# An expert-dispatch kernel on one core: eight groups of 16 tokens in place of nine groups of 15 and 14, with the last group also stored in two pieces

## The chip, the cores and the metric

The kernel runs on one core of a Trainium2 chip, with the other cores idle. The metric is the device time of one execution in microseconds (us). The kernel before takes 242.47 us, the median of three runs (242.39 to 246.49).

## What is computed

Each of 16 x 1024 tokens is a row of 512 float32 numbers. The reference repeats the row k = 2 times and multiplies each copy by one of the token's two weights. The expert indices are not used.

```python
x_expanded = x[:, :, np.newaxis, :].repeat(k, axis=2)      # (16, 1024, 2, 512)
weights = expert_weights[..., np.newaxis]                  # (16, 1024, 2, 1)
return (x_expanded * weights).astype(np.float32)
```

33.6 MB are read, 67.1 MB are written, and one multiplication is made for each number written.

## The kernel before

The 16,384 tokens are spread over 128 partitions, 128 tokens on each, and worked off in groups. A group of T takes 128 x T neighbouring tokens; partition p holds T tokens that lie next to each other in memory (`rows`), so that one partition's share of a load is one run of T x 2 KB and of a store one run of T x 4 KB. `groups` (line 30) is [15, 15, 14, 14, 14, 14, 14, 14, 14].

**Slots.** There are three slots (`slots`, bufs=3), each as large as the output of the largest group. Input and output share a slot: `load` (lines 112 to 124) puts the input into the last half of the part that the group uses, and the products are written from the front. `ranges` (lines 127 to 135) cuts a group so that no product overwrites input that is still needed: the first VectorE instruction takes about half of the tokens, the next half of what is left, and so on, down to all tokens but the last. `products` (line 140) is one VectorE multiplication with both weights of each token broadcast along the row. The last token's two products are made by ScalarE in `last` (line 157), since their place is that of the input itself.

**Weights.** The weights are loaded in long rows by `weights_in` (line 68, on the SP queue) and spread over the partitions by `weights_spread`: TensorE transposes blocks of columns (line 84), VectorE copies them out in another order (line 89), TensorE transposes back (line 95), and VectorE writes `w_tile` (line 100). Since a weights load has the same group size throughout, there are two: one for the two groups of 15, one for the seven groups of 14. Every product needs the `w_tile` columns of its group.

**Order.** The order of the work is the order of the program on each engine (a manual schedule). All token loads are issued on the ScalarE queue, all stores and the weights loads on the SP queue. At the start the two weights loads and the loads of groups 0, 1 and 2 are issued; the load of group 0 is two transfers of 7 and 8 tokens. Then, for each group: the VectorE products, the two ScalarE products, and the store (line 184). For group 0 alone, the output of the first VectorE product is stored on its own as soon as it is there (line 180), and the rest by line 184. After group i (from group 1 on) the load of group i + 2 is issued; it goes into the slot of group i - 1, and so waits until the store of that group has landed. It waits on the ScalarE queue, behind the two products of group i and ahead of those of group i + 1.

Of the kernel before, what the change touches and what calls it, by code (L numbers as in the profile page):

```python
# [1 line left out]

# [4 lines left out]


@with_exitstack
def kernel(  # L10
    ctx: ExitStack,
    tc: tile.TileContext,
    x: bass.AP,
    expert_indices: bass.AP,
    expert_weights: bass.AP,
    out: bass.AP,
):
    nc = tc.nc

    batch, seq, hidden = x.shape  # L20
    k = expert_weights.shape[-1]
    P = nc.NUM_PARTITIONS
    ntok = batch * seq
    assert ntok % P == 0

    f32 = mybir.dt.float32
    row = k * hidden


    groups = [15, 15, 14, 14, 14, 14, 14, 14, 14]  # L30
    assert sum(groups) * P == ntok
    TX = max(groups)

    xf = x.rearrange("b s h -> (b s) h")
    of = out.rearrange("b s k h -> (b s) (k h)")
    wf = expert_weights.rearrange("b s k -> (b s) k")

    w_pool = ctx.enter_context(tc.tile_pool(name="w_pool", bufs=1))
    slots = ctx.enter_context(tc.tile_pool(name="slots", bufs=3))
    raw_pool = ctx.enter_context(tc.tile_pool(name="raw_pool", bufs=1))  # L40
    psum = ctx.enter_context(
        tc.tile_pool(name="psum", bufs=2, space=bass.MemoryType.PSUM)
    )

    w_tile = w_pool.tile([P, sum(groups) * k], f32)

    def rows(flat, done, T):
        return flat[done * P : (done + T) * P, :].rearrange("(p a) n -> p (a n)", a=T)

    B = 8
    M = P // B
    ident = w_pool.tile([P, P], f32)
    nc.gpsimd.memset(ident, 0.0)  # L55
    nc.gpsimd.affine_select(  # L56
        out=ident,
        in_=ident,
        compare_op=mybir.AluOpType.not_equal,
        fill=1.0,  # L60
        base=0,
        pattern=[[-1, P]],
        channel_multiplier=1,
    )

    def weights_in(head, G, T):
        raw_tile = raw_pool.tile([G * M, B * T * k], f32, name=f"raw{T}_tile")
        nc.sync.dma_start(  # L68
            out=raw_tile,
            in_=wf[head * P : (head + G * T) * P, :].rearrange(  # L70
                "(q a) n -> q (a n)", a=B * T
            ),
        )
        return raw_tile

    def weights_spread(raw_tile, head, G, T):
        n = T * k
        col_tile = raw_pool.tile([n, G * P], f32, name=f"col{T}_tile")
        cols = col_tile.rearrange("c (q r) -> c q r", r=B)
        step = 4  # L80
        for r0 in range(0, B, step):
            up_tile = psum.tile([n, step, G * M], f32)
            for r in range(step):
                nc.tensor.transpose(  # L84
                    up_tile[:, r, :],
                    raw_tile[:, (r0 + r) * n : (r0 + r + 1) * n],
                    ident[: G * M, : G * M],
                )
            nc.vector.tensor_copy(  # L89
                out=cols[:, :, r0 : r0 + step],  # L90
                in_=up_tile.rearrange("c r q -> c q r"),
            )
        down_tile = psum.tile([P, G * n], f32)
        for g in range(G):
            nc.tensor.transpose(  # L95
                down_tile[:, g * n : (g + 1) * n],
                col_tile[:, g * P : (g + 1) * P],
                ident[:n, :n],
            )
        nc.vector.tensor_copy(  # L100
            out=w_tile[:, head * k : (head + G * T) * k], in_=down_tile
        )

    ctx.enter_context(tc.manual_schedule())

    starts = [sum(groups[:i]) for i in range(len(groups))]
    loaded = []

    def load(i):
        if i >= len(groups):
            return
        T = groups[i]
        slot_tile = slots.tile([P, TX * row], f32)
        loaded.append(slot_tile)
        src = rows(xf, starts[i], T)
        at = T * (row - hidden)
        for lo, hi in [(0, T // 2), (T // 2, T)] if i == 0 else [(0, T)]:  # L120
            nc.scalar.dma_start(
                out=slot_tile[:, at + lo * hidden : at + hi * hidden],
                in_=src[:, lo * hidden : hi * hidden],
            )


    def ranges(T):
        lo, out = 0, []
        while lo < T - 1:
            hi = lo + 1  # L130
            while (hi + 1) * k <= T * (k - 1) + lo and hi < T - 1:
                hi += 1
            out.append((lo, hi))
            lo = hi
        return out

    def products(slot_tile, T, lo, hi, w_at):
        m = hi - lo
        at = T * (row - hidden) + lo * hidden
        nc.vector.tensor_tensor(  # L140
            out=slot_tile[:, lo * row : hi * row].rearrange(
                "p (t k h) -> p t k h", t=m, k=k
            ),
            in0=slot_tile[:, at : at + m * hidden]
            .rearrange("p (t h) -> p t h", t=m)
            .unsqueeze(2)
            .to_broadcast([P, m, k, hidden]),
            in1=w_tile[:, w_at + lo * k : w_at + hi * k]
            .rearrange("p (t k) -> p t k", t=m)
            .unsqueeze(3)  # L150
            .to_broadcast([P, m, k, hidden]),
            op=mybir.AluOpType.mult,
        )

    def last(slot_tile, T, w_at):
        for c in range(T * k - k, T * k):
            nc.scalar.mul(  # L157
                out=slot_tile[:, c * hidden : (c + 1) * hidden],
                in_=slot_tile[:, T * row - hidden : T * row],
                mul=w_tile[:, w_at + c : w_at + c + 1],  # L160
            )

    raw15 = weights_in(0, 2, 15)
    raw14 = weights_in(30, 7, 14)
    load(0)
    load(1)
    load(2)
    weights_spread(raw15, 0, 2, 15)
    weights_spread(raw14, 30, 7, 14)

    for i, T in enumerate(groups):
        slot_tile = loaded[i]
        outr = rows(of, starts[i], T)
        w_at = starts[i] * k
        done = 0
        for lo, hi in ranges(T):
            products(slot_tile, T, lo, hi, w_at)
            if i == 0 and done == 0:
                done = hi
                nc.sync.dma_start(  # L180
                    out=outr[:, : done * row], in_=slot_tile[:, : done * row]
                )
        last(slot_tile, T, w_at)
        nc.sync.dma_start(
            out=outr[:, done * row :], in_=slot_tile[:, done * row : T * row]
        )
        if i:
            load(i + 2)

# [1 line left out]
_INS = ['x', 'expert_indices', 'expert_weights']  # L191
_OUTS = [((16, 1024, 2, 512), 'float32')]


# [23 lines left out]
```

## Time and profile before

| | before |
|---|---|
| median of the runs | 242.47 us (242.39, 242.47, 246.49) |
| profiled execution, its own time | 242.25 us |
| span of that execution, from first to last instruction | 240.4 us |
| moved by DMA | 100.80 MB |
| loads of x | 10 transfers, ScalarE queue (q10) |
| stores | 10 transfers, SP queue (q1, with 2 loads of weights) |

All numbers of the trace come from the one profiled execution. The span is 1.85 us shorter than its time. An instruction group's line gives, after the shapes and the count, the busy time in us and the mean ns of one instruction, and then the idle time ahead of it with what ended most of it. In the table of stretches (start:end in us, length) the engines' busy times are followed by the granted TensorE clock (1.00 throughout), the mean busy share of the 16 DMA engines, and the GB/s moved; a DMA packet is counted whole where it starts, so short stretches can stand above 1.00 or too low. "DMA to landing" is the time from the issue of a transfer until its completion is seen. In the chain of waits a line is: start, length, what ran or was waited for.

### The profile page before, as it was taken

Reading aid. Unit: us, or ns where it says so; the run is one execution under the profiler, and the core shown is the slowest. Engines: PE = TensorE matmul, PEld = TensorE weight load, DVE = VectorE, ACT = ScalarE, POOL = GpSimd, SP = SyncE. Lnnn points to the kernel's source line nnn. Section 1 sums busy time; section 2 is a strip of 40 time slices with the busy share of each in tenths; the row PEclk is TensorE's granted clock in tenths of the full one; section 3 lists DMA queues with packets and bytes.
Section 4 is the critical chain, followed back from the end, with each engine's and each line's share of the span. In section 5 each row is a group of like instructions: output and inputs, shape, how many; then the busy total and the mean of one; then the engine's idle time right before and its main releaser. Section 6 shows DMA issues by size and latency. Waiting matters only on the chain.

```text
span 240.4 us, 221 instructions
## 1 busy us (share of the span) xinstructions
PE 3.6 (1%) x25; PEld 2.5 (1%) x25; DVE 134.7 (56%) x42; ACT 14.3 (6%) x19; POOL 0.7 (0%) x6
## 2 busy tenths in 40 slices
PE   1210000000000000000000000000000000000000
PEld 1110000000000000000000000000000000000000
DVE  1189999998000697079605980399019930895000
ACT  0020010200100002000200011000200020002000
POOL 1000000000000000000000000000000000000000
DMA  7999999999799899899999997998999998897897
GB/s 268 464 434 392 382 458 414 436 491 480 316 480 458 382 458 458 382 448 391 458 525 391 458 458 310 453 458 386 453 458 458 458 458 382 382 458 305 363 401 305
DMA packets 3056, 100.80 MB, mean 419 GB/s; under 512 B 352, under 2 KB 496, under 8 KB 496
## 3 DMA queue, kind: packets, MB, share of 16 engines
q1 hardware_dynamic: 1616, 67.24, 64.7%
q10 hardware_dynamic: 1440, 33.56, 32.9%
HBM read 33.69 MB, written 67.11 MB: 419 GB/s over the span
## 4 chain that ended last, share of the span: by engine, by line
DMA 57%; DVE 31%; ACT 2%; PE 1%; issue 1%; SPq 0%; DVEq 0%
DVE slot_tile L140 31%; DMA out_dram<-slot_tile 29%; DMA slot_tile<-in_x_dram 24%; DMA raw_tile<-in_expert_weights_dram 4%; ACT slot_tile L157 2%; PE up_tile L84 1%; PE down_tile L95 0%; DVE col_tile L89 0%; SPq L68 0%; DVEq L140 0%; DVE w_tile L100 0%
## 5 line engine op out<-in xcount | busy, mean ns | idle before, releaser
L140 DVE TENSOR_TENSOR slot_tile<-slot_tile,w_tile 128x7168 f32<-128x7168 f32 (+4 forms) x36 | 132.5, 3684 | 73.4 <-DMA slot_tile<-in_x_dram 72.5
L157 ACT ACTIVATE slot_tile<-slot_tile,w_tile 128x512 f32<-128x512 f32 x18 | 13.0, 721 | 194.2 <-DVE slot_tile L140 193.9
L89 DVE COPY col_tile<-up_tile 30x128 f32<-30x128 f32 (+1 forms) x4 | 1.7, 445 | 10.0 <-PE up_tile L84 9.9
L84 PE MATMUL up_tile<-ident,raw_tile 32*30 32x32 f32 (+1 forms) x16 | 2.2, 308 | 8.8 <-DMA raw_tile<-in_expert_weights_dram 8.8
L157 ACT ACT_TABLE_LOAD x1 | 1.3, 1283 | 12.7 <-DMA slot_tile<-in_x_dram 12.7
L84 PEld LDWEIGHTS up_tile<-ident,raw_tile 32*30 32x30 f32 (+1 forms) x16 | 1.4, 124 | 9.1 <-issue 8.9
L100 DVE COPY w_tile<-down_tile 128x60 f32<-128x60 f32 (+1 forms) x2 | 0.6, 291 | 1.5 <-PE down_tile L95 1.5
L95 PE MATMUL down_tile<-ident,col_tile 28*128 28x28 f32 (+1 forms) x9 | 1.4, 288 | 1.1 <-DVE col_tile L89 1.1
L95 PEld LDWEIGHTS down_tile<-ident,col_tile 28*128 28x128 f32 (+1 forms) x9 | 1.1, 210 | 1.7 <-DVE col_tile L89 1.7
L56 POOL TENSOR_SCALAR_AFFINE_SELECT ident<-ident 128x128 f32<-128x128 f32 x1 | 0.3, 292 | 0.1
L55 POOL MEMSET ident<- 128x128 f32 x1 | 0.2, 205 | 0.3 <-POOLq L202 0.3
L202 POOL MEMSET const-bfloat16-1.0<- 128x1 bf16 x1 | 0.1, 101 | 0.0
L202 POOL MEMSET const-uint8-127<- 128x1 uint8 x1 | 0.1, 101 | 0.0
L202 POOL MEMSET const-float32-0.0<- 128x1 f32 x1 | 0.1, 98 | 0.2 <-issue 0.2
L202 POOL MEMSET const-float32-1.0<- 128x1 f32 x1 | 0.1, 98 | 0.0
## 6 DMA issues: line engine op xcount, KB each, us to landing
out_dram<-slot_tile SPq DMA_DIRECT2D x7, 7168.0 KB, 31.3
slot_tile<-in_x_dram ACTq DMA_DIRECT2D x7, 3584.0 KB, 29.7
out_dram<-slot_tile SPq DMA_DIRECT2D x1, 7680.0 KB, 27.0
out_dram<-slot_tile SPq DMA_DIRECT2D x1, 4096.0 KB, 18.1
slot_tile<-in_x_dram ACTq DMA_DIRECT2D x1, 3840.0 KB, 20.1
out_dram<-slot_tile SPq DMA_DIRECT2D x1, 3584.0 KB, 18.0
slot_tile<-in_x_dram ACTq DMA_DIRECT2D x1, 2048.0 KB, 11.5
slot_tile<-in_x_dram ACTq DMA_DIRECT2D x1, 1792.0 KB, 6.9
```

Of the source, the lines that this page charges most:

```text
L55: nc.gpsimd.memset(ident, 0.0)
L56: nc.gpsimd.affine_select(out=ident, in_=ident, compare_op=mybir.AluOpType.not_equal, fill=1.0, base=0, pattern=[[-1, P]], channel_multipl ...
L84: nc.tensor.transpose(up_tile[:, r, :], raw_tile[:, (r0 + r) * n : (r0 + r + 1) * n], ident[: G * M, : G * M],)
L89: nc.vector.tensor_copy(out=cols[:, :, r0 : r0 + step], in_=up_tile.rearrange("c r q -> c q r"),)
L95: nc.tensor.transpose(down_tile[:, g * n : (g + 1) * n], col_tile[:, g * P : (g + 1) * P], ident[:n, :n],)
L100: nc.vector.tensor_copy(out=w_tile[:, head * k : (head + G * T) * k], in_=down_tile)
L140: nc.vector.tensor_tensor(out=slot_tile[:, lo * row : hi * row].rearrange("p (t k h) -> p t k h", t=m, k=k), in0=slot_tile[:, at : at + m ...
L157: nc.scalar.mul(out=slot_tile[:, c * hidden : (c + 1) * hidden], in_=slot_tile[:, T * row - hidden : T * row], mul=w_tile[:, w_at + c : w_ ...
L202: nc = _bacc.Bacc("TRN2", target_bir_lowering=False, num_devices=1)
```

## The change

The groups become eight of 16 tokens. A slot is then 16 x 4 KB = 64 KB on each partition, and one partition's run is 32 KB of a load and 64 KB of a store. Since all groups have one size, one weights load of 128 rows and one spreading take the place of two. The load of group 0 becomes one transfer. The store of the last group is made in two pieces, as that of group 0 already is.

```diff
-    groups = [15, 15, 14, 14, 14, 14, 14, 14, 14]
+    groups = [16] * 8
...
-        for lo, hi in [(0, T // 2), (T // 2, T)] if i == 0 else [(0, T)]:
-            nc.scalar.dma_start(
-                out=slot_tile[:, at + lo * hidden : at + hi * hidden],
-                in_=src[:, lo * hidden : hi * hidden],
-            )
+        nc.scalar.dma_start(out=slot_tile[:, at : at + T * hidden], in_=src)
...
-    raw15 = weights_in(0, 2, 15)
-    raw14 = weights_in(30, 7, 14)
+    raw_tile = weights_in(0, 8, 16)
     load(0)
     load(1)
     load(2)
-    weights_spread(raw15, 0, 2, 15)
-    weights_spread(raw14, 30, 7, 14)
+    weights_spread(raw_tile, 0, 8, 16)
...
-            if i == 0 and done == 0:
+            if i in (0, len(groups) - 1) and done == 0:
                 done = hi
                 nc.sync.dma_start(
                     out=outr[:, : done * row], in_=slot_tile[:, : done * row]
```

## Prediction

> **What bounds the kernel now.** I read the page from the top: busy shares, then slices, then DMA queues.
>
> ```profile
> span 240.4 us, 221 instructions
> PE 3.6 (1%) x25; PEld 2.5 (1%) x25; DVE 134.7 (56%) x42; ACT 14.3 (6%) x19; POOL 0.7 (0%) x6
> DMA  7999999999799899899999997998999998897897
> DMA packets 3056, 100.80 MB, mean 419 GB/s; under 512 B 352, under 2 KB 496, under 8 KB 496
> q1 hardware_dynamic: 1616, 67.24, 64.7%
> q10 hardware_dynamic: 1440, 33.56, 32.9%
> ```
>
> VectorE is busy for 56% of the span, the two DMA queues together for 64.7 + 32.9 = 97.6%. So the 16 DMA engines bound the kernel, and only 2.4%, 5.8 us, is theirs to lose. A slice counts a packet where it starts, so single digits jump; I therefore asked for stretches, cut where I suspected idle time. The last two columns are the DMA share and GB/s.
>
> ```profile
> 0.00:2.60 2.60, 0.00 (x0) 0.00 (x0) 0.00 (x0) 0.00 (x0) 0.70 (x6) 1.00 0.42 89
> 2.60:99.00 96.40, 3.59 (x25) 2.54 (x25) 62.17 (x22) 7.05 (x9) 0.00 (x0) 1.00 1.00 429
> 99.00:176.00 77.00, 0.00 (x0) 0.00 (x0) 43.50 (x12) 4.33 (x6) 0.00 (x0) 1.00 1.01 435
> 176.00:219.10 43.10, 0.00 (x0) 0.00 (x0) 28.46 (x8) 1.44 (x2) 0.00 (x0) 1.00 0.98 426
> 219.10:222.00 2.90, 0.00 (x0) 0.00 (x0) 0.54 (x1) 1.44 (x2) 0.00 (x0) 1.00 0.00 0
> 222.00:239.20 17.20, 0.00 (x0) 0.00 (x0) 0.00 (x0) 0.00 (x0) 0.00 (x0) 1.00 0.99 427
> 239.20:240.40 1.20, 0.00 (x0) 0.00 (x0) 0.00 (x0) 0.00 (x0) 0.00 (x0) 1.00 0.00 0
> ```
>
> This table is the argument. From 2.6 to 219.1 us the transfers run without a hole at 426 to 435 GB/s. Idle are some 1.5 us at the start, 1.2 us at the end, and one hole of 2.9 us at 219.1. What makes the hole stands in the chain of waits and in the timeline:
>
> ```profile
> 176.36 28.56 DMA slot_tile<-in_x_dram
> 204.91 0.03 issue
> ...
> 205.04 7.64 DVE slot_tile L140
> ...
> 219.68 0.73 ACT slot_tile L157
> ```
> ```profile
> 195.75 0.33 SPq L184 DMA_DIRECT2D out_dram<-slot_tile  x1
> ```
> ```profile
> DMA to landing us min/median/max: 23.9/23.9/23.9
> ```
> ```profile
> 221.18 0.33 SPq L184 DMA_DIRECT2D out_dram<-slot_tile  x1
> ```
>
> The last load lands at 204.9. The store before the last was issued at 195.75 and lands 23.9 us later, at 219.65: at 204.9 there are 14.7 us of it left. The last group needs 16.2 us from load to the issue of its store (221.18), and that store's first bytes move at 222.0, 0.8 us after the issue. No other transfer exists by then. That is the hole.
>
> **The change, part by part.** Bytes first. Loads, stores and weights move the same bytes (100.66 MB of rows; 30 + 98 KB of weights become 128 KB). Work of the bound resource is therefore unchanged but for packets; the time can only fall by holes that close.
>
> *The last store in two pieces.* The products of one group, by form:
>
> ```profile
> L140 DVE TENSOR_TENSOR slot_tile<-slot_tile,w_tile 128x7168 f32<-128x7168 f32 x9 | 68.6, 7623 | 72.5 <-DMA slot_tile<-in_x_dram 72.5
> L140 DVE TENSOR_TENSOR slot_tile<-slot_tile,w_tile 128x2048 f32<-128x2048 f32 x9 | 20.6, 2292 | 0.3
> L157 ACT ACTIVATE slot_tile<-slot_tile,w_tile 128x512 f32<-128x512 f32 x18 | 13.0, 721 | 194.2 <-DVE slot_tile L140 193.9
> L140 DVE TENSOR_TENSOR slot_tile<-slot_tile,w_tile 128x1024 f32<-128x1024 f32 x9 | 11.0, 1225 | 0.3
> L140 DVE TENSOR_TENSOR slot_tile<-slot_tile,w_tile 128x4096 f32<-128x4096 f32 x2 | 8.9, 4426 | 0.1
> ```
>
> With T = 16 `ranges` gives (0,8), (8,12), (12,14), (14,15): outputs of 8192, 4096, 2048 and 1024. From 4096 to 7168 the cost grows by (7623 - 4426) / 3072 = 1.04 ns an element, so 8192 takes 7623 + 1024 x 1.04 = 8.69 us. One group: 8.69 + 4.43 + 2.29 + 1.23 + 0.07 of gaps = 16.7 us on VectorE, then two ScalarE products, 1.49 us with gaps. Let X be the landing of the last load. What is left of the store before it scales with the group: 14.7 x 16/14 = 16.8 us. The first piece (4.19 MB) is issued at X + 0.1 + 8.7 = X + 8.8 and could move at X + 9.6: 7.2 us before the engines run dry. It keeps them until 16.8 + 4.19 MB / 432 GB/s = X + 26.5. The second piece is issued at X + 0.1 + 16.7 + 1.5 = X + 18.3 and could move at X + 19.1, 7.4 us early. The hole is gone: -2.9 us. Without the split it would stay: X + 19.1 against X + 16.8 less the 0.5 us from last byte to landing (239.0 to 239.5) is 2.8 us, so larger groups alone bring nothing here. On SP the added wait (first product of the last group) has behind it only the second piece; nothing else queues there. Its issue costs 0.4 us of SP, idle then.
>
> *Groups of 16 in the steady part.* Eight loads and stores take the place of nine, in three slots. Does a store come late for its predecessor? Before, with rows above and these:
>
> ```profile
> 170.40 0.33 SPq L184 DMA_DIRECT2D out_dram<-slot_tile  x1
> ```
> ```profile
> 145.02 31.32 DMA out_dram<-slot_tile
> ```
>
> the store of 145.02 lands at 176.34, so the next, issued at 170.40, is 5.9 us early. The distance is two periods less a load and a group: 2 x 25.4 - 28.6 - 16.2 = 6.0. With 16: period 25.4 x 8/7 = 29.0, load 28.6 x 8/7 = 32.7, group 18.3, and 58.0 - 51.0 = 7.0 us early. The cover gets thicker; cost nothing. If the cover failed, each us of lateness would be a us of hole in each of five periods.
>
> *One weights load and one first load.* They set when the first product starts:
>
> ```profile
> 1.16 8.89 DMA raw_tile<-in_expert_weights_dram
> ...
> 13.81 7.63 DVE slot_tile L140
> ```
> ```profile
> 12.71 1.28 ACT L157 ACT_TABLE_LOAD   x1 [12.71 <-DMA slot_tile<-in_x_dram]
> ```
> ```profile
> raw_tile<-in_expert_weights_dram SPq DMA_DIRECT2D x1, 30.0 KB, 2.2
> ```
> ```profile
> 49.17 0.33 ACTq L121 DMA_DIRECT2D slot_tile<-in_x_dram  x1
> ```
> ```profile
> 46.58 14.85 SPq L184 DMA_DIRECT2D out_dram<-slot_tile  x2
> ```
>
> Today the second weights load lands at 10.05 and the spreading takes 3.76 us more; with 128 columns in place of 112 and eight second transposes in place of seven I add 0.5 us (3.76 x 1/7). The first weights load, ahead of the tokens, took 2.2 us; the second, between them, 8.9. The merged one lies between landing at 3 us and, if each of its eight rows an engine waits for one token row, landing with the whole first load: 12.71 + 0.262 MB / 432 GB/s = 13.3. First product then: no earlier than 13.3 (the load), no later than 13.3 + 4.3 = 17.6. I take about 14, because the merged load is issued where the fast one was and is no longer second in line. What hangs on it is the store of group 1. Before, store 0 has landed when the fourth load goes out, 49.17, and store 1 was issued at 46.58. After, 80 token units of 0.262 MB go ahead of it in place of 74 (48 loaded, 16 stored twofold): 49.2 + 1.57 MB / 432 GB/s = 52.8. Store 1 is issued at the first product + 2 x 16.72 + 1.5 = + 34.9: 48.9 for 14, 52.5 for 17.6. It must be out 0.8 + 0.5 us before 52.8, at 51.5; so the cost is 0 up to a first product at 16.6 and 1.0 us at the far bound. I take 0. Two DMA issues fewer on SP and ACT (0.4 to 0.7 us each) lie ahead of nothing late.
>
> *Packets.* From the queue lines: stores 155.5 us for 67.24 MB, 2.313 us per MB at 24.0 packets per MB; loads 79.1 us for 33.56 MB, 2.357 at 42.9. A packet costs at most 0.044 / 18.9 = 0.0023 us. A transfer of 128 rows is 128 packets and 16 completions (10 loads on q10: 1440). Two loads fewer are 288 packets, one weights load fewer 32; stores stay ten. 3056 becomes 2736: 0 to -0.7 us. I take -0.2, near zero, because the loads' excess also holds the slow start (89 GB/s in the first row of stretches). A store row becomes 65,536 B, longer than any of this trace (61,440). Should it be cut in two, 768 packets are added: up to +1.8 us.
>
> *Row pitch.* Rows of one tile now lie 32 KB (loads) and 64 KB (stores) apart in HBM, both powers of two; here they lie 28, 30, 56 and 60 KB apart, so no row prices it. The nearest on the good side is 435 GB/s (99 to 176 us), on the bad side the slowest stretch that is fully busy:
>
> ```profile
> 2.60:28.20 25.60, 3.59 (x25) 2.54 (x25) 16.54 (x9) 1.28 (x1) 0.00 (x0) 1.00 1.00 416
> ```
>
> which is 3.7% under 432. On 233 us that is +8.6 us; on the other side -0.7%, -1.6 us. I take 0: loads and stores, with pitches a factor of two apart, run at one rate, so here the DMA engines and not HBM set it.
>
> The Trainium skill, DMA: Bandwidth & Descriptors (section Latency and other measured facts), warns that copies lose rate when the row pitch is a large power of two: 207 GB/s per direction at 512 KiB against 214 in full, 103 at 4 MiB. As an estimate from that page, its 3% would add 7 us and give 246.4; its smallest pitch is eight times ours, and no row here shows one.
>
> **Sum.** Against the profiled execution (242.25 us, of which 1.85 lie outside the span): 242.25 - 2.9 - 0.2 = 239.15. That execution is 0.2 below the median of 242.47, so on the median's scale 239.4, -1.3%.
>
> **Rivals.**
> *Power-of-two pitch slows every transfer* (the other side). For it: the pitches are new. Against: one rate for all pitches seen. At the 416 GB/s bound 239.4 + 8.6 = 248.0, slower by 2.3%. It cancels the gain from 1.3% on and passes the 2% from 3.4% on.
> *The hole stays.* It would, if the second product waited for the first piece's store to read the slot, or the piece were issued only with the rest. Against: store 0 is cut alike, and its VectorE chain shows no such wait (13.81 + 7.63 is followed by a product at 21.46). Time 242.3.
> *Every transfer pays its own start.* Three fewer transfers (22 to 19) would then save three times the 0.8 + 0.5 us of the last store, 3.9 us more: 235.5. Against: the share of 1.00 for 216 us has no room for any start; they lie under other transfers. The Trainium skill, SBUF — State Buffer (section The DMA setup-cost knee), states a fixed 2 us for every transfer; by that, 6 us would go and the time be 233.4, while the stretches show it only where a transfer is alone.
> *A late first product or rows cut in two.* +1.0 or +1.8 us: 240.4 to 241.2.
>
> ```profile
> 21.43 0.02 issue
> 21.46 4.44 DVE slot_tile L140
> ```
>
> **How the numbers follow.** Forecast 0.74 (238.4 to 240.2 for itself); pitch 0.12, two thirds of it above 247.3; hole stays 0.05; own starts 0.04; late start or cut rows 0.05. The range 238.4 to 242.5 takes in the forecast, the stayed hole and the small losses, 0.84, and leaves out pitch and own starts. Faster by over 2% (under 237.6) 0.04, slower by over 2% 0.08, within 2% 0.88; 2% is about what a measurement tells from no change.
>
> **What would show it.** Right: a DMA share near 1.00 from 2.6 us to within 2 us of the end; the first piece of the last store issued some 9.5 us before the second, neither with idle engines ahead of it; 2736 packets; the large product near 8.69 us; stores issued 7 us ahead of their predecessor's landing. Wrong: a rate below 426 GB/s at full share (pitch), more packets (cut rows), or a zero stretch near 50 us or ahead of the last stores.

## The result and the profile after

The changed kernel takes 0.988 of the time before (95% interval 0.984 to 0.991): 239.18 to 239.43 us in five of its 16 runs and 241.52 in a sixth, against 242.36 to 242.54 us in seven of 16 and 244.04 in an eighth. The profiled execution took 239.30 us with a span of 237.5. The other runs, ten of the changed kernel (243.90 to 250.12 us) and eight of the one before (246.15 to 251.33), were in a slower state, which the ratio leaves out; with them the medians are 247.22 and 245.09 us.

The page of the changed kernel, its span and the DMA lines:

```profile
span 237.5 us, 184 instructions
DMA packets 2736, 100.80 MB, mean 424 GB/s; under 512 B 304, under 2 KB 432, under 8 KB 432
q1 hardware_dynamic: 1584, 67.24, 65.5%
q10 hardware_dynamic: 1152, 33.55, 33.2%
```

The queues are now busy for 98.7% of the span, up from 97.6%. In us that is 98.7% of 237.5, 234.4 of packets after, and 97.6% of 240.4, 234.6 before: the same work, with less idle time around it. The stretches show where (start:end, length, engines, then clock, DMA share, GB/s):

```profile
2.60:99.00 96.40, 2.92 (x16) 1.93 (x16) 66.15 (x18) 5.61 (x7) 0.00 (x0) 1.00 1.01 432
99.00:176.00 77.00, 0.00 (x0) 0.00 (x0) 39.99 (x11) 4.33 (x6) 0.00 (x0) 1.00 0.99 429
176.00:217.00 41.00, 0.00 (x0) 0.00 (x0) 28.53 (x8) 1.44 (x2) 0.00 (x0) 1.00 1.00 435
217.00:222.00 5.00, 0.00 (x0) 0.00 (x0) 0.02 (x1) 1.44 (x2) 0.00 (x0) 1.00 0.97 419
222.00:236.10 14.10, 0.00 (x0) 0.00 (x0) 0.00 (x0) 0.00 (x0) 0.00 (x0) 1.00 0.95 409
236.10:237.50 1.40, 0.00 (x0) 0.00 (x0) 0.00 (x0) 0.00 (x0) 0.00 (x0) 1.00 0.00 0
```

The stretch from 217 to 222 us is the one to look at. The last ScalarE product runs in it, and before, nothing moved beside that; now 419 GB/s do. The timeline of the last group, and the landing of the store ahead of it (issued at 189.55, by its line alone):

```profile
200.28 16.74 DVE L136 TENSOR_TENSOR slot_tile<-slot_tile,w_tile 128x8192 f32<-128x8192 f32 x4 [12.27 <-DMA slot_tile<-in_x_dram]
209.00 0.33 SPq L174 DMA_DIRECT2D out_dram<-slot_tile  x1
217.05 1.48 ACT L153 ACTIVATE slot_tile<-slot_tile,w_tile 128x512 f32<-128x512 f32 x2 [27.53 <-DVE slot_tile L136]
218.55 0.33 SPq L178 DMA_DIRECT2D out_dram<-slot_tile  x1
```
```profile
189.55 0.33 SPq L178 DMA_DIRECT2D out_dram<-slot_tile  x1
```
```profile
DMA to landing us min/median/max: 27.5/27.5/27.5
```

The store ahead lands at 189.55 + 27.5 = 217.05. The first piece has been waiting in the queue since 209.00 and follows it without a gap; it in turn covers the second piece, issued at 218.55.

### The profile page after: what moved, and what is told of

It is laid out like the page before. It is cut to its first block, busy times and chain, and to the rows that moved or that the text cites. A ratio compares the mean times of both kernels' runs of the same rounds, so it can differ in the third digit from the quotient of the medians.

```text
span 237.5 us, 184 instructions
## 1 busy us (share of the span) xinstructions
PE 2.9 (1%) x16; PEld 1.9 (1%) x16; DVE 134.7 (57%) x35; ACT 12.8 (5%) x17; POOL 0.7 (0%) x6
## 2 busy tenths in 40 slices
DMA packets 2736, 100.80 MB, mean 424 GB/s; under 512 B 304, under 2 KB 432, under 8 KB 432
## 4 chain that ended last, share of the span: by engine, by line
DMA 61%; DVE 28%; ACT 2%; issue 0%; DVEq 0%; ACTq 0%
DMA slot_tile<-in_x_dram 33%; DMA out_dram<-slot_tile 29%; DVE slot_tile L136 28%; ACT slot_tile L153 2%; DVEq L136 0%; ACTq L120 0%
## 5 line engine op out<-in xcount | busy, mean ns | idle before, releaser
L136 DVE TENSOR_TENSOR slot_tile<-slot_tile,w_tile 128x8192 f32<-128x8192 f32 (+3 forms) x32 | 132.9, 4158 | 71.6 <-DMA slot_tile<-in_x_dram 70.7
L153 ACT ACTIVATE slot_tile<-slot_tile,w_tile 128x512 f32<-128x512 f32 x16 | 11.5, 721 | 192.5 <-DVE slot_tile L136 192.3
L89 DVE COPY col_tile<-up_tile 32x512 f32<-32x512 f32 x2 | 1.4, 678 | 9.6 <-PE up_tile L84 9.6
L84 PE MATMUL up_tile<-ident,raw_tile 128*32 128x128 f32 x8 | 1.9, 411 | 8.4 <-DMA raw_tile<-in_expert_weights_dram 8.4
L84 PEld LDWEIGHTS up_tile<-ident,raw_tile 128*32 128x32 f32 x8 | 1.0, 135 | 8.8 <-issue 8.4
L95 PE MATMUL down_tile<-ident,col_tile 32*128 32x32 f32 x8 | 1.1, 292 | 0.8 <-DVE col_tile L89 0.8
L95 PEld LDWEIGHTS down_tile<-ident,col_tile 32*128 32x128 f32 x8 | 0.9, 214 | 1.3 <-DVE col_tile L89 1.3
## 6 DMA issues: line engine op xcount, KB each, us to landing
slot_tile<-in_x_dram ACTq DMA_DIRECT2D x8, 4096.0 KB, 32.6
```

The lines of the kernel that those rows point to most:

```text
L84: nc.tensor.transpose(up_tile[:, r, :], raw_tile[:, (r0 + r) * n : (r0 + r + 1) * n], ident[: G * M, : G * M],)
L89: nc.vector.tensor_copy(out=cols[:, :, r0 : r0 + step], in_=up_tile.rearrange("c r q -> c q r"),)
L95: nc.tensor.transpose(down_tile[:, g * n : (g + 1) * n], col_tile[:, g * P : (g + 1) * P], ident[:n, :n],)
L136: nc.vector.tensor_tensor(out=slot_tile[:, lo * row : hi * row].rearrange("p (t k h) -> p t k h", t=m, k=k), in0=slot_tile[:, at : at + m ...
L153: nc.scalar.mul(out=slot_tile[:, c * hidden : (c + 1) * hidden], in_=slot_tile[:, T * row - hidden : T * row], mul=w_tile[:, w_at + c : w_ ...
```

## Experiments

All start from the kernel before or the changed one. Five kernels were run in two sets, and both are given. The trace keeps the start and length of every DMA packet and the 16 completions of every transfer, one from each DMA engine; where the text says "packet records" or "completions", the numbers come from there.

**Which part brings the gain: the second cut alone.** The kernel before with one line of the change:

```diff
-            if i == 0 and done == 0:
+            if i in (0, len(groups) - 1) and done == 0:
```

> The kernel before with one edit: the store of its last group (14 tokens) is made in two pieces. Theory (the gain is the hole ahead of the last store and nothing else): 242.4 - 2.9 = 239.5 us, a span near 237.6, and no stretch of DMA share 0 between 2.6 us and the last byte. Rival (the gain comes from fewer and larger transfers): this kernel has one transfer more than before, so it stays at 242.4 us or rises.

> Once more the kernel before with the store of its last group made in two pieces and nothing else, because some DMA engines fell behind for parts of the first run, whatever the kernel. Theory (the hole is the whole gain): 239.5 us. Rival (fewer and larger transfers bring it): 242.4 us.

The first set gave 243.59 to 246.47 us, ratio 1.013 (1.003 to 1.022), which is neither expected value. In the second, three of four runs took 239.23 to 239.60 us: ratio 0.988 (0.986 to 0.990), the same as for the whole change. The profiled execution of that set took 243.11 us, but the place of the hole can be read in it. Its last group and its stretches:

```profile
209.28 14.61 DVE L140 TENSOR_TENSOR slot_tile<-slot_tile,w_tile 128x7168 f32<-128x7168 f32 x4 [11.30 <-DMA slot_tile<-in_x_dram]
216.93 0.33 SPq L180 DMA_DIRECT2D out_dram<-slot_tile  x1
225.41 0.33 SPq L184 DMA_DIRECT2D out_dram<-slot_tile  x1
```
```profile
219.10:222.00 2.90, 0.00 (x0) 0.00 (x0) 2.87 (x2) 0.00 (x0) 0.00 (x0) 1.00 1.06 455
222.00:236.00 14.00, 0.00 (x0) 0.00 (x0) 1.85 (x2) 1.44 (x2) 0.00 (x0) 1.00 0.99 426
236.00:240.20 4.20, 0.00 (x0) 0.00 (x0) 0.00 (x0) 0.00 (x0) 0.00 (x0) 1.00 0.10 41
```

No stretch ahead of the last bytes stands empty: 426 GB/s right through the issue of the last piece (225.41). In the trace of the first set there is no such stretch either (a share of 0.94 from 219.1 to 222.0 us). The row at 236 shows trailing engines, that is, engines that end after the others: a share of 0.10 for 4 us, which the packet records show to be three engines of 16 at work, then two, then one. This kernel has 23 transfers, the most of the four variants of groups and cut, and is as fast as the changed kernel with 19. So the smaller number of transfers is not where the gain is.

**The other part alone: groups of 16, last group stored whole.**

```diff
-            if i in (0, len(groups) - 1) and done == 0:
+            if i == 0 and done == 0:
```

> The changed kernel with the last group stored whole, so eight groups of 16, one weights load and one first load, without the second cut. Theory (the gain is the hole and nothing else): the hole is there, 2.8 us long, behind the landing of the store before the last; 242.2 us, a span near 240.3. Rival (fewer and larger transfers bring the gain): 239.3 to 240 us.

> Once more the changed kernel with the last group stored whole. Theory (the hole is the whole gain): 242.2 us with a hole of 2.8 us ahead of the last store. Rival (fewer and larger transfers bring it): 239.3 to 240 us.

Eleven of the twelve runs of the two sets lie between 249.3 and 256.9 us, which neither side expected; one took 242.08 us, 0.1 from the 242.2 of the theory and 2.1 us above the most that the rival allows. One run is thin evidence for the size of the gain. The hole itself shows in the trace of the second set (own time 250.42 us):

```profile
208.61 16.74 DVE L136 TENSOR_TENSOR slot_tile<-slot_tile,w_tile 128x8192 f32<-128x8192 f32 x4 [14.28 <-DMA slot_tile<-in_x_dram]
```
```profile
226.88 0.33 SPq L178 DMA_DIRECT2D out_dram<-slot_tile  x1
```
```profile
217.20:227.70 10.50, 0.00 (x0) 0.00 (x0) 8.04 (x4) 1.44 (x2) 0.00 (x0) 1.00 0.16 69
225.00:227.60 2.60, 0.00 (x0) 0.00 (x0) 0.34 (x1) 1.44 (x2) 0.00 (x0) 1.00 0.00 0
227.70:247.20 19.50, 0.00 (x0) 0.00 (x0) 0.00 (x0) 0.00 (x0) 0.00 (x0) 1.00 1.00 430
```

The last load took 35.2 us to land (32.6 in the changed kernel). Its first completion came at 197.94 and its last at 208.48, and only then did the first product start (208.61); in the changed kernel the 16 completions of the last load lie within 0.4 us. Most engines had done their part of the store ahead by 217 and ran dry, while VectorE was still at the last group; the slowest went on to 225. From 225.0 to 227.6 no engine moved anything, until the first bytes of the store issued at 226.88. By the packet records the stretch without any engine is 2.8 us long, as the theory has it, and 2.7 us at the same place in the trace of the first set (own time 250.32 us). The 10.5 us of the row above are longer because the engines did not end together; what made them uneven is not shown.

**How late may the first product come?** The weights load is issued behind two token loads, on the ScalarE queue:

```diff
-        nc.sync.dma_start(
+        nc.scalar.dma_start(
             out=raw_tile,
...
-    raw_tile = weights_in(0, 8, 16)
     load(0)
     load(1)
+    raw_tile = weights_in(0, 8, 16)
     load(2)
```

> The changed kernel with the weights load issued on the ScalarE queue behind the loads of groups 0 and 1. The weights then land near 23.3 us (the first load lands at 13.1, the second about 9.7 later, the weights behind it) and the first product starts near 23.3 + 4.3 = 27.6 in place of 13.2. Theory (a late first product is free up to a start near 16.6, then each us is a us of hole): 27.6 - 16.6 = 11 us more, 250.3 us, with idle DMA engines between 32 and 64 us, in two holes. Rival (the queues are deep enough and the time is bytes over rate): 239.3 us.

251.70 us in the lowest run, which is the profiled one, and 255.57 to 256.78 in the other three. The first product starts at 27.39, and the two holes are there:

```profile
31.80:37.00 5.20, 0.00 (x0) 0.00 (x0) 5.17 (x2) 0.00 (x0) 0.00 (x0) 1.00 0.07 32
37.20:56.40 19.20, 0.00 (x0) 0.00 (x0) 19.10 (x5) 1.44 (x2) 0.00 (x0) 1.00 0.95 410
56.50:63.20 6.70, 0.00 (x0) 0.00 (x0) 6.63 (x4) 1.44 (x2) 0.00 (x0) 1.00 0.25 68
63.40:248.00 184.60, 0.00 (x0) 0.00 (x0) 97.09 (x24) 8.65 (x12) 0.00 (x0) 1.00 1.00 429
```

The first ends with the start of the first piece of store 0, the second with store 1. The rows are 5.2 and 6.7 us long; since some packets fall inside them, the idle time in them, averaged over the engines, is 11.3 us by the packet records, against the 11 expected. This one late start fits the allowance for the first product (free up to about 16.6 us, then us for us); where exactly the free part ends was not tested. The weights of the change, landing near 8, use none of it.

**Lateness in the steady part, four groups long and once.** The first product of a group is made again, into the same place; the output stays what it is:

```diff
             for lo, hi in ranges(T):
-                products(slot_tile, T, lo, hi, w_at)
+                for _ in range(2 if i in (3, 4, 5, 6) and lo == 0 else 1):
+                    products(slot_tile, T, lo, hi, w_at)
```

> The changed kernel with the first VectorE product of groups 3, 4, 5 and 6 made twice (the same product into the same place), 8.7 us more of VectorE in each of these four groups; VectorE then works 25.4 us in a period of 29. The stores of these groups were issued 7.0 us ahead of the landing of the store before, of which 1.3 us are landing and start, so each is now 3.0 us late. Theory of the prediction (each us of lateness is a us of hole in each period): 4 x 3.0 = 12 us more, 251.3 us. Rival (a hole lets the next load run alone and land earlier, so that the next group is early again; the lateness is paid only in every other period): 3.2 us more, 242.5 us, in two holes of 1.6 us. Second rival (DMA work is never short of something to move): 239.3 us.

> Once more the changed kernel with the first product of groups 3 to 6 made twice. Theory of the prediction (each us of lateness a us of hole in each period): 251.3 us, four holes. Rival (a hole is paid in every other period, since the next load then lands earlier): 242.5 to 244.5 us, two holes; the first run showed two, of 3.0 and 2.0 us, which would be 239.3 + 5.0 = 244.3.

The runs took 244.72 to 251.60 us (first set) and 246.35 to 253.31 us (second), so that times alone don't decide. The traces do. That of the first set (own time 247.70 us) has two holes, not four:

```profile
110.80:115.40 4.60, 0.00 (x0) 0.00 (x0) 3.95 (x3) 1.44 (x2) 0.00 (x0) 1.00 0.51 164
```
```profile
115.40:203.00 87.60, 0.00 (x0) 0.00 (x0) 73.96 (x15) 2.88 (x4) 0.00 (x0) 1.00 0.99 425
203.30:205.20 1.90, 0.00 (x0) 0.00 (x0) 1.09 (x1) 1.23 (x2) 0.00 (x0) 1.00 0.00 0
```

The idle time in them, averaged over the engines, is 3.0 and 2.0 us by the packet records. Between them lie 88 us at full share, although two of the four lengthened groups fall there. The second set's trace (own time 251.11 us) has its two holes at the same places, with 3.9 and 4.4 us of idle time:

```profile
110.30:115.00 4.70, 0.00 (x0) 0.00 (x0) 3.64 (x3) 1.44 (x2) 0.00 (x0) 1.00 0.42 126
115.40:203.00 87.60, 0.00 (x0) 0.00 (x0) 71.03 (x14) 2.88 (x4) 0.00 (x0) 1.00 0.99 420
203.60:209.00 5.40, 0.00 (x0) 0.00 (x0) 4.32 (x3) 1.44 (x2) 0.00 (x0) 1.00 0.51 218
```

The timeline of the first set shows how the kernel mends itself:

```profile
113.61 0.34 ACTq L120 DMA_DIRECT2D slot_tile<-in_x_dram  x1
114.35 90.57 SPq L179 DMA_DIRECT2D out_dram<-slot_tile  x4
138.92 1.48 ACT L153 ACTIVATE slot_tile<-slot_tile,w_tile 128x512 f32<-128x512 f32 x2 [24.60 <-DVE slot_tile L136]
141.34 25.47 DVE L136 TENSOR_TENSOR slot_tile<-slot_tile,w_tile 128x8192 f32<-128x8192 f32 x5 [2.45 <-DMA slot_tile<-in_x_dram]
```

The load issued at 113.61, ahead of the late store (114.35), lands by 141.3, after 27.7 us in place of 32.6. It was issued 0.7 us ahead of that store; in the changed kernel the store has been waiting for 7 us by then (131.51 and 138.49). So its group starts 5 us earlier than it would have, which is more than the 3.0 us of lateness. The prediction's sentence that a failed cover costs in every period is wrong. The self-correcting rival is right in the number of holes. It is wrong in their place, since it expected one in every other period and they came at the stores of groups 3 and 6, with two late groups between them that cost nothing. And it is low in size: 3.2 us expected, 5.0 of idle time.

The same with three products in group 3 only:

```diff
-                products(slot_tile, T, lo, hi, w_at)
+                for _ in range(3 if i == 3 and lo == 0 else 1):
+                    products(slot_tile, T, lo, hi, w_at)
```

> The changed kernel with the first VectorE product of group 3 alone made three times, 17.4 us more of VectorE once. Theory (lateness beyond the 5.7 us of cover is a hole, once): 17.4 - 5.7 = 11.7 us of hole near 112 us, 251.0 us; by the rival of self-correction, in which the next load lands earlier behind a hole, the hole comes once as well, 10 to 12 us, and no second one follows. If DMA work is never short: 239.3 us.

253.61 us in the lowest run, the profiled one, ratio to before 1.051 (1.040 to 1.062); the others took 255.85 to 258.85. In the profiled one, one engine ends some 2 us after the rest. One hole, and none after it:

```profile
110.30:121.00 10.70, 0.00 (x0) 0.00 (x0) 10.60 (x5) 1.44 (x2) 0.00 (x0) 1.00 0.15 43
121.40:247.00 125.60, 0.00 (x0) 0.00 (x0) 63.64 (x16) 5.77 (x8) 0.00 (x0) 1.00 1.00 429
```

10.7 us against 11.7 expected. So of the 17.4 us of extra work some 7 were covered, a little more than the 5.7 expected, and the lateness beyond that is paid once.

**Row pitch.** Each partition takes 128 consecutive tokens, so that the rows of one tile lie 256 KB (loads) and 512 KB (stores) apart; the weights need no transposes then:

```diff
-        return flat[done * P : (done + T) * P, :].rearrange("(p a) n -> p (a n)", a=T)
+        wide = flat.rearrange("(p a) n -> p (a n)", p=P)
+        n = flat.shape[-1]
+        return wide[:, done * n : (done + T) * n]
...
-    raw_tile = weights_in(0, 8, 16)
+    nc.sync.dma_start(out=w_tile, in_=wf.rearrange("(p a) n -> p (a n)", p=P))
...
-    weights_spread(raw_tile, 0, 8, 16)
```

> The changed kernel with another layout of the tokens: partition p holds tokens 128 p to 128 p + 127, so that the rows of one tile lie 256 KB (loads) and 512 KB (stores) apart in HBM in place of 32 and 64 KB; run lengths, sizes and order of the transfers stay. The weights then lie in the order in which the products read them, and are loaded straight into place; the transposes go. Theory (the DMA engines set the rate, whatever the pitch): 239.3 us, with a rate of 430 to 435 GB/s at full share. Rival (large power-of-two pitches slow HBM): by the rule weighed in the prediction some 3% on 233 us, 7 us more, 246 us, at 417 GB/s.

> Once more the changed kernel with partition p holding tokens 128 p to 128 p + 127 (rows of a tile 256 and 512 KB apart, weights loaded straight into place, no transposes), because some DMA engines fell behind for parts of the first run, whatever the kernel. Theory (the DMA engines set the rate whatever the pitch): 239.3 us. Rival (large power-of-two pitches slow HBM by some 3%): 246 us.

All twelve runs lie between 246.47 and 248.61 us (ratios to before 1.018, 1.014 to 1.022, and 1.022, 1.018 to 1.025), while runs of the kernel before beside them reached 242.3. The second set's profile:

```profile
2.60:99.00 96.40, 60.32 (x14) 5.61 (x7) 0.00 (x0) 1.00 1.00 425
99.00:176.00 77.00, 39.30 (x11) 4.33 (x6) 0.00 (x0) 1.00 1.00 419
176.00:219.00 43.00, 26.43 (x6) 1.44 (x2) 0.00 (x0) 1.00 1.00 423
219.00:236.00 17.00, 6.84 (x3) 1.44 (x2) 0.00 (x0) 1.00 0.98 424
236.00:244.00 8.00, 0.00 (x0) 0.00 (x0) 0.00 (x0) 1.00 0.50 217
```

Full share, but 419 to 425 GB/s in place of 429 to 435, and at the end 8 us at a mean share of 0.50, in which the engines end one after the other.

The Trainium skill, DMA: Bandwidth & Descriptors (section Latency and other measured facts), gives 207 GB/s for copies at a row pitch of 512 KiB against 214 in full, about 3% less; 246.5 / 239.2 is 3.1%. The time agrees with that rule.

But the packet records do not show a pitch that slows every transfer. The usual (median) packet of 32 KB takes 1.213 us and that of 64 KB 2.418 us here, just as in the changed kernel. What is different is that 274 of 2304 packets take over 2% longer than the usual one, up to 3.25 us, where the changed kernel's trace has 39. Such packets are not peculiar to these pitches: the doubled products, with the pitches of the change, have 161 and 157 in their two traces, and 420 GB/s from 115.4 to 203 us in the second. Whether the wide pitches make them more frequent stays open, and with it the cause of the 7 us. What is shown is that the pitches of the change, 32 and 64 KB, cost nothing: per KB its usual packets take as long as those of 28 and 56 KB before (1.062 and 2.116 us).

**Number of transfers.** Every load and every whole store is cut into two:

```diff
-        nc.scalar.dma_start(out=slot_tile[:, at : at + T * hidden], in_=src)
+        for lo, hi in [(0, T // 2), (T // 2, T)]:
+            nc.scalar.dma_start(
+                out=slot_tile[:, at + lo * hidden : at + hi * hidden],
+                in_=src[:, lo * hidden : hi * hidden],
+            )
...
-        nc.sync.dma_start(
-            out=outr[:, done * row :], in_=slot_tile[:, done * row : T * row]
-        )
+        for lo, hi in [(done, T)] if done else [(0, T // 2), (T // 2, T)]:
+            nc.sync.dma_start(
+                out=outr[:, lo * row : hi * row],
+                in_=slot_tile[:, lo * row : hi * row],
+            )
```

> The changed kernel with every load and every whole store cut into two transfers, issued one behind the other: 33 transfers in place of 19, 14 more, the same bytes; a load row is then 16 KB a packet, a store row 32 KB. Theory (starts lie under other transfers): no holes; 2016 packets more at 0 to 0.0023 us each, 0 to 4.6 us by the bound, and 1 us as I take it from the -0.2 us taken for 320 packets: 240.3 us. Rival (every transfer pays its own start of 0.8 + 0.5 us): + 14 x 1.3 = 18 us, 257 us.

> Once more the changed kernel with every load and every whole store cut into two transfers, 33 in place of 19, because some DMA engines fell behind for parts of the first run, whatever the kernel. Theory (starts lie under other transfers, a packet has a small price): 240.3 us, no holes before the last byte. Rival (every transfer pays its own start): 257 us; the lowest run of the first set, 246.3, speaks against it already, but leaves open a price of up to 7 us for 14 more transfers.

Lowest runs 246.27 and 246.23 us, the others up to 253.11; ratios to before 1.025 (1.015 to 1.035) and 1.029 (1.021 to 1.036). That is neither 240.3 nor 257. The second set's profiled execution is its lowest run:

```profile
219.00:236.00 17.00, 0.00 (x0) 0.00 (x0) 0.00 (x0) 0.00 (x0) 0.00 (x0) 1.00 1.00 432
236.00:242.80 6.80, 0.00 (x0) 0.00 (x0) 0.00 (x0) 0.00 (x0) 0.00 (x0) 1.00 0.30 130
```
```profile
span 244.1 us, 224 instructions
q1 hardware_dynamic: 2448, 67.24, 64.7%
q10 hardware_dynamic: 2304, 33.56, 32.8%
```

There is no empty stretch until 236 us, where the last bytes of the changed kernel come as well: a start is not paid by each transfer. The rule of the Trainium skill, SBUF — State Buffer (section The DMA setup-cost knee), by which each pays 2 us (28 for these 14, as an estimate), is not borne out where the queues are full: the whole difference is 7 us. But packet time is (64.7 + 32.8)% of 244.1 = 238.0 us, 3.6 more than in the changed kernel, and then 6.8 us follow at a share of 0.30 in which some engines finish alone. The packet records divide the 3.6 us. A usual packet of 16 KB takes 0.611 us, of 32 KB 1.213 and of 64 KB 2.418, so two halves take 0.008 to 0.009 us more than the whole on their engine; over all the packets and 16 engines that is 1.0 us, as the theory had it. The rest is for the most part in packets that took over 2% longer than the usual one, 215 of 4096. So the price of the shorter packets is as expected, and the time above 240.3 us comes of slow packets and of engines that end late. Whether cutting the transfers brings these about is not shown.

## Why the prediction was right, and where it was not

- *Only holes can close.* Right. Packet time went from 234.6 to 234.4 us; the span fell by 2.9 us, the length of the hole. One line, the second cut, gives the same 0.988 as the whole change. The time alone would not have shown this, since the range took in 242.3 us, the time with the hole, as well; the stretches and that one line do.
- *The last store.* Right to 0.1 us: 16.9 us of the store ahead were left at the landing of the last load (217.05 - 200.16; 16.8 predicted); the pieces were issued 8.84 and 18.39 us after it (8.8 and 18.3). The margins of 7.2 and 7.4 us ahead of the moment when the engines run dry are counted to a landing; by the prediction's own 0.5 us from last byte to landing they are that much smaller, which changes nothing. The 8192 product took 8.69 us, as extrapolated:

```profile
L136 DVE TENSOR_TENSOR slot_tile<-slot_tile,w_tile 128x8192 f32<-128x8192 f32 x8 | 69.5, 8691 | 70.7 <-DMA slot_tile<-in_x_dram 70.7
```

- *Steady part.* Right in cover: the store of 160.55 was issued 7.0 us ahead of the landing of the one before (131.51 + 36.0 = 167.51), 7.0 predicted. Wrong in what stands behind the cover: a late store does not cost in each of the periods, as the doubled products show: two holes for four late groups.

```profile
131.51 36.00 DMA out_dram<-slot_tile
```
```profile
160.55 0.33 SPq L178 DMA_DIRECT2D out_dram<-slot_tile  x1
```

- *The start.* Right that it costs nothing. The merged weights load landed 7.5 us after its issue, inside the bounds, and so the first token load, not the weights, sets the first product: 13.21, against the 14 that I took. Store 0 had landed when the next load went out, at 52.81; 52.8 was predicted.

```profile
13.21 50.03 DVE L136 TENSOR_TENSOR slot_tile<-slot_tile,w_tile 128x8192 f32<-128x8192 f32 x12 [0.66 <-DMA slot_tile<-in_x_dram]
52.81 0.33 ACTq L120 DMA_DIRECT2D slot_tile<-in_x_dram  x1
```

- *Packets.* 2736, as counted. By the usual packet times, the smaller number saves 0.1 us, near the 0.2 taken. The end after the last byte took 1.4 us in place of 1.2, and the profiled execution 239.30 us against 239.15. The upper bound of 0.0023 us a packet held and was far too high, as the prediction suspected: one more packet takes 0.008 to 0.009 us of one engine, 0.0005 us of 16. In the changed kernel's trace all 39 packets that are over 2% longer than usual are loads of the first 26 us, so what the bound took for a price of packets is for the most part the slow start.
- *Pitch.* The value 0 was right for 32 and 64 KB. The reason given for it, that the DMA engines set the rate whatever the pitch, was argued from pitches up to 60 KB, and the runs at 256 and 512 KB leave open whether it reaches that far.

## What to carry to other kernels

Where the DMA queues are full, cut the timeline into stretches by DMA share and look for the ones at zero: one line that fills such a stretch was worth the whole change here, and larger groups with fewer transfers added nothing to it that these runs can tell. The place to look is the last group, whose compute has nothing behind it; storing its first half early covers the second half. Measure a cover by how early a transfer is issued before its predecessor lands, less start and landing (5.7 us here, where some 7 were in fact covered), and don't multiply a lateness by the number of periods before asking whether the next load gains from it.

## What was not expected of the hardware

A transfer has landed only when the slowest engine has done its share, and an engine that has fallen behind does not catch up while the queues are full. With the last group stored whole (second set), the first and last completion of one and the same load lie 2.6, 4.3, 8.5 and 10.5 us apart in the last four loads. A hole evens the engines out: in the first trace of the doubled products they lie 2.2 us apart for the load that lands at 113.4 us, at the hole, and 0.6 us apart for the next one. Without a hole the difference shows at the end, as the rows with a share of 0.10 over 4.2 us, 0.30 over 6.8 us and 0.50 over 8.0 us do. In these traces single packets take longer than the usual one (up to 3.25 us in place of 2.418); why they do stays open.
